# Three of a pair's seven low parts formed in PSUM by a matmul with a negated identity

## The chip, the cores and the metric

The kernel runs on one core of a Trainium2 chip. The metric is the device time of one execution in microseconds (us); shown are the median and the ends of several runs. One further execution was taken by the hardware profiler; its span goes from the first to the last instruction.

## What is computed

One inference step of a small streaming encoder: 1024 prompt tokens and 8 x 16 sample tokens, model width 1024, two layers. Layer 0 has sliding-window attention, layer 1 chunked attention on a shared K/V; each ends in an output projection and an MLP. What matters here, cut from the reference:

```python
def rmsnorm(x, g):
    y = xf * lax.rsqrt(jnp.mean(xf * xf, axis=-1, keepdims=True) + EPS)
    return (y * g.astype(jnp.float32)).astype(x.dtype)

def mlp(x, g_norm, w_up, w_down):
    return jnp.square(jax.nn.relu(rmsnorm(x, g_norm) @ w_up)) @ w_down

        hp = hp + ap @ w_o_a[i]
        hp = hp + mlp(hp, g_mlp[layer], w_up[layer], w_down[layer])
```

All is in float32 and has to be accurate, so the kernel splits each factor of a product into a high and a low part and adds three matmuls.

## The kernel before

**High and low parts.** TensorE multiplies in a shorter format (fp32r). `split` (L107 to L115) writes the high part with a copy that rounds to that format, by ScalarE unless told otherwise (L109), and the low part as source minus high part, by VectorE (L115). A product is three matmuls: high by high, high by low, low by high (L715 to L717 in the MLP, L147 to L149 in the output projection).

**The stage around the change.** `wo_phase` runs once in each layer, between attention and the MLP. It takes the nine tiles of 128 tokens (eight of the prompt, ST of the sample) in the order of WO_ORDER. For each, M(t) adds attention times output weights to x (L653, by VectorE from the bank ps_wo), stores x (L655, a DMA that ScalarE issues) and norms it in place: a square with a sum by ScalarE (L605), two small operations, and the scaling of x by VectorE (L610), which overwrites what the store reads. `load_o` splits attention's output (tiles oh and ol).

**Pairs and parts.** The MLP multiplies 2 x 2 blocks with seven products instead of eight. So as soon as tile i and tile i + 4 are done, S(i) forms four sums and differences of their halves on GpSimd (tiles s; L669 to L672), and T(i) turns seven parts p = 0 to 6, each 128 tokens by 512: the halves x1 low, x1 high, x2 high, then the four sums. There are four pairs in a layer, i = 0 to 3. `turn` transposes a part on TensorE in four pieces into one PSUM bank (ps_n, three banks in turn, L662), ScalarE copies the high part out of it into sx (L109), VectorE subtracts the low part into sx (L115), and the bank is free. The sample's tile is turned in two parts of its own.

**What follows.** `mlp_up` starts with a block of its own kind: the first 256 tokens of each half (pairs 0 and 1) and then the other 256, so that TensorE has products while the last pairs are turned. Its products go 0, 1, 5, ...: the first fills ps_x, which ScalarE copies (hc, L834); the second fills ps_z, which VectorE adds (L836); the third adds to ps_x and is copied (L839), and so on. The block's weights are loaded (ru), combined by VectorE (L775 to L778) and split (w, wq) by the same two engines.

**What sets the order.** Each engine works through its own queue in order. The queues are not written by hand here: a scheduler deals the instructions of the whole program to the queues, by a timeline that it works out and by priorities; the products of the MLP are tied to their order. So a change of one step can deal the instructions around it anew.

Of the kernel before, what the change touches and what calls it, by code (L numbers as in the profile page):

```python
# [9 lines left out]
F32R = mybir.dt.float32r  # L10
AF = mybir.ActivationFunctionType
ALU = mybir.AluOpType
# [4 lines left out]
P = 128  # L17
# [58 lines left out]
class Build:  # L76
# [535 lines left out]
    def wo_phase(self, layer, sx, x8, wo):  # L612
        nc = self.nc
        with ExitStack() as st:
            self.psum_pools(st, f"wo{layer}", dict(m=(4, 1), g=(3, 1)), dict(m="m", n="g"))
            work = self.pool(st, f"wow{layer}")
            small = self.pool(st, f"wosm{layer}", 2)
            osp, xs = {}, {}
            lo, hi = slice(0, 512), slice(512, 1024)

            def O(t, z):
                if t in self.kept:
                    xs[t] = self.kept[t]
                    return
                if len(xs) % 5 < 2:
                    xs[t] = self.rawp.tile([P, D], F32, tag="raw", name="x")
                else:
                    xs[t] = work.tile([P, D], F32, tag="x", name="x", bufs=3)
                nc.sync.dma_start(xs[t], self.xd[t])
                if t in self.wo_done:  # L630
                    return
                with self.tc.high_priority(WO_PRIO) if len(osp) < 2 else nullcontext():
                    load_o(t, z)

            def second():
                self.last = work.tile([P, 4, P], F32, tag="o2", name="o2")
                return self.last

            def load_o(t, z):
                o = work.tile([P, 4, P], F32, tag=f"o{z}", name="o")  # L640
                self.load_halves(layer, 1, t, o, second, nc.vector)
                oh = work.tile([P, 4, P], F32R, tag=f"oh{z}", name="oh")
                ol = work.tile([P, 4, P], F32R, tag=f"ol{z}", name="ol")
                self.split(oh, ol, o)
                osp[t] = oh, ol

            def M(t):
                x = xs[t]
                for n in range(2) if t not in self.wo_done else ():
                    nn = slice(n * 512, n * 512 + 512)  # L650
                    ps = self.psum("m", [P, 512], "ps_wo")
                    self.wo_proj(ps, *osp[t], wo, nn)
                    nc.vector.tensor_tensor(x[:, nn], ps, x[:, nn], ALU.add)  # L653
                if t not in self.wo_done:
                    nc.scalar.dma_start(self.xd[t], x)  # L655
                if t not in self.kept:
                    self.norm(small, work.tile([P, D], mybir.dt.bfloat16, tag="junk", name="junk"), x)

            def turn(src, dst, c, d):
                ps = self.psum("n", [P, 4, P], "ps_n")  # L660
                for k in range(4):
                    nc.tensor.transpose(ps[:, k, :], src[:, k * P : (k + 1) * P], self.ident)  # L662
                self.split(dst[0][:, d, c], dst[1][:, d, c], ps)

            def S(i):
                x1, x2 = xs[i], xs[i + NT // 2]
                s = self.sums() if i else self.sums0
                tt = nc.gpsimd.tensor_tensor
                tt(s[0], x2[:, lo], x2[:, hi], ALU.add)  # L669
                tt(s[1], s[0], x1[:, lo], ALU.subtract)  # L670
                tt(s[2], x1[:, lo], x2[:, lo], ALU.subtract)
                tt(s[3], x1[:, hi], s[1], ALU.subtract)  # L672
                return [x1[:, lo], x1[:, hi], x2[:, hi], *s]

            def T(i, src):
                c = slice(i * P, i * P + P)
                for p in (0, 1, 2, 3, 4, 5, 6):
                    turn(src[p], sx[p], c, slice(0, 4))

            order = WO_ORDER[layer]  # L680
            ready, pend = set(), []
            z = 0
            for t in order[:2]:
                O(t, z % 2)
                z += t not in self.wo_done
            for n, t in enumerate(order):
                if n + 2 < NTILE:
                    O(order[n + 2], z % 2)
                    z += order[n + 2] not in self.wo_done
                M(t)  # L690
                ready.add(t)
                for f in pend:
                    f()
                pend = []
                if t == ST:
                    def sample():
                        for h in range(2):
                            turn(xs[ST][:, h * 512 : h * 512 + 512], x8, slice(0, P), slice(4 * h, 4 * h + 4))
                    pend.append(sample)
                elif (t + 4) % NT in ready:  # L700
                    i = t % 4
                    T(i, S(i))
            for f in pend:
                f()
# [1094 lines left out]
```

## Time and profile before

| | |
|---|---|
| runs | 2407.91 us median of 3 (2406.41 to 2412.36) |
| profiled execution, span | 2399.3 us |
| TensorE / weight loads busy | 2320.4 us (97%) / 1935.5 us (81%) |
| VectorE / ScalarE / GpSimd busy | 1626.3 us (68%) / 1217.9 us (51%) / 535.6 us (22%) |
| mean granted TensorE clock | 0.992 |
| output projection of layer 0 and of layer 1, with the turns | about 397 to 457 us and 1642 to 1692 us |

No time of its own is given for the profiled execution beside its span; the runs were timed apart from it. In the rows of the profile PE is TensorE, PEld its weight loads, DVE VectorE, ACT ScalarE, POOL GpSimd and SP SyncE; L12 is line 12 of the kernel. A row of the timeline has start, length, engine, line, operation, and in brackets the idle time before it with what ended it. A row of the groups has count, busy us, mean ns of one, then the idle time before them. A row of the waits has who waited for whom, us in total, times, and the longest. A row of the stretches has length, then busy us of PE, PEld, DVE, ACT and POOL with the number of instructions, the granted clock, the share of the DMA engines and GB/s.

### The profile page before, as it was taken

The page shows a single profiled execution, that of the slowest core. Times are in us where ns is not written, and L with a number is a line of the kernel's source. Part 1 is how long each engine was busy: PE and PEld are TensorE (multiplying, and loading weights), DVE is VectorE, ACT ScalarE, POOL GpSimd, SP SyncE. Part 2 cuts the span into 40 slices and gives each one's busy share as a digit, 9 for nine tenths or more (in the row PEclk, how much of TensorE's full clock was granted, in tenths as well). Part 3 has the DMA queues.
Part 4 walks back from the last instruction along what each step waited for, and adds up shares of the span by engine and source line. Part 5 has one row for each costly group of instructions (what it writes and reads, how often), then busy time and mean ns, then how long its engine had stood idle before and what let it go on. Part 6 is the DMA issues. An engine that isn't in the chain of part 4 may idle for free.

```text
span 2399.3 us, 33421 instructions
## 1 busy us (share of the span) xinstructions
PE 2320.4 (97%) x11621; PEld 1935.5 (81%) x11621; DVE 1626.3 (68%) x3002; ACT 1217.9 (51%) x2423; POOL 535.6 (22%) x828
## 2 busy tenths in 40 slices
PE   7998999899999999999999999998999999999999
PEld 6786877788888888888777788887888888888887
DVE  6687786755655777776567877877655555776674
ACT  4676675555555433232267666665655555333321
POOL 3343332312112100000333434344211211000000
PEclk9998999999999999999999999999999999999999
DMA  7345546244433874342743555555434435744332
GB/s 244 122 127 168 171 156 200 95 155 158 145 128 141 323 245 146 117 141 99 237 149 111 188 161 173 173 169 174 138 127 145 154 137 200 278 140 158 112 116 114
DMA packets 218457, 385.88 MB, mean 161 GB/s; under 512 B 50408, under 2 KB 125104, under 8 KB 211120
## 3 DMA queue, kind: packets, MB, share of 16 engines
q1 hardware_dynamic: 195136, 307.16, 39.0%
q0 software_dynamic: 21776, 71.84, 7.7%
q10 hardware_dynamic: 1376, 4.74, 0.5%
q8 instruction: 92, 1.51, 0.3%
q14 instruction: 77, 0.63, 0.1%
HBM read 246.47 MB, written 136.14 MB: 159 GB/s over the span
## 4 chain that ended last, share of the span: by engine, by line
PE 82%; DMA 7%; DVE 5%; ACT 2%; issue 2%; POOL 1%; SPq 1%; ACTq 0%; DVEq 0%; POOLq 0%
PE ps_x L715 9%; PE ps_x L717 9%; PE ps_x L716 9%; PE ps_y L717 7%; PE ps_y L716 7%; PE ps_y L715 7%; PE ps_mm L186 3%; PE ps_mm L188 3%; PE ps_mm L187 3%; PE ps_tr L293 2%; PE ps_mm L147 2%; PE ps_mm L149 2%; PE ps_mm L148 2%; PE ps_s L717 1%; PE ps_s L716 1%
## 5 line engine op out<-in xcount | busy, mean ns | idle before, releaser
L109 ACT CAST w<-r 128x2048 fp32r<-128x2048 f32 x56 | 107.1, 1913 | 322.9 <-PE ps_y L717 212.1
L715 PE MATMUL ps_x<-w,s 128*128 128x512 f32 x512 | 199.5, 390 | 2.7 <-DVE hc L854 2.1
L717 PE MATMUL ps_x<-w,s 128*128 128x512 f32 x512 | 199.4, 389 | 0.0
L716 PE MATMUL ps_x<-w,s 128*128 128x512 f32 x512 | 199.2, 389 | 0.0
L186 PE MATMUL ps_mm<-w,hh 128*128 128x512 f32 x432 | 175.0, 407 | 13.8 <-ACT kw L253 5.1
L188 PE MATMUL ps_mm<-w,hl 128*128 128x512 f32 x432 | 174.3, 403 | 1.7 <-DMA hl<-hTd 1.4
L187 PE MATMUL ps_mm<-w,hh 128*128 128x512 f32 x432 | 172.5, 400 | 0.7 <-DVE w L159 0.7
L109 ACT CAST s<-s 128x2048 fp32r<-128x2048 f32 x56 | 107.1, 1913 | 117.9 <-DMA s<-hd 108.6
L115 DVE TENSOR_TENSOR w<-r,w 128x2048 fp32r<-128x2048 f32 x56 | 128.2, 2290 | 51.9 <-ACT w L109 51.9
L715 PE MATMUL ps_x<-sx,w 128*128 128x512 f32 (+1 forms) x408 | 157.8, 387 | 4.6 <-ACT hc L834 2.7
L1021 DVE TENSOR_TENSOR x<-ps_y,x 128x512 f32<-128x512 f32 x136 | 92.3, 687 | 101.1 <-PE ps_y L717 101.0
L717 PE MATMUL ps_x<-sx,w 128*128 128x512 f32 (+1 forms) x408 | 154.1, 378 | 0.0
L716 PE MATMUL ps_x<-sx,w 128*128 128x512 f32 (+1 forms) x408 | 154.1, 378 | 0.0
L109 ACT CAST w<-ru 128x512 fp32r<-128x512 f32 (+1 forms) x160 | 110.0, 708 | 85.3 <-PE ps_y L716 32.0
L717 PE MATMUL ps_y<-w,s 128*128 128x512 f32 x384 | 149.5, 389 | 0.0
L716 PE MATMUL ps_y<-w,s 128*128 128x512 f32 x384 | 149.4, 389 | 0.0
L715 PE MATMUL ps_y<-w,s 128*128 128x512 f32 x384 | 149.4, 389 | 0.0
L115 DVE TENSOR_TENSOR s<-s 128x2048 fp32r<-128x2048 f32 x56 | 128.1, 2287 | 26.5 <-ACT s L109 26.5
L115 DVE TENSOR_TENSOR ptl<-ps_tr,pth 128x512 fp32r<-128x512 f32 x180 | 122.6, 685 | 24.8 <-ACT pth L109 19.0
L115 DVE TENSOR_TENSOR w<-ru,w 128x512 fp32r<-128x512 f32 (+1 forms) x160 | 126.6, 793 | 10.9 <-ACT w L109 10.8
L109 ACT CAST pth<-ps_tr 128x512 fp32r<-128x512 f32 x180 | 104.8, 594 | 47.9 <-PE ps_tr L293 39.3
L115 DVE TENSOR_TENSOR wq<-ru,wq 128x1024 fp32r<-128x1024 f32 x32 | 39.7, 1240 | 131.9 <-ACT wq L109 131.9
(280 smaller groups left out, 6573.3 us busy)
## 6 DMA issues: line engine op xcount, KB each, us to landing
s<-hd SPq DMA_DIRECT2D x56, 1024.0 KB, 4.7
ru<-in_w_up SPq DMA_DIRECT2D x64, 512.0 KB, 3.9
r<-in_w_down SPq DMA_DIRECT2D x32, 1024.0 KB, 5.7
hd<-hc POOLq DMA_DIRECT2D x128, 256.0 KB, 2.7
hd<-hs POOLq DMA_DIRECT2D x96, 256.0 KB, 2.5
x<-xd SPq DMA_DIRECT2D x41, 512.0 KB, 4.6
o<-oTd SPq DMA_DIRECT2D x52, 256.0 KB, 4.1
hTd<-hh SPq DMA_DIRECT2D x36, 256.0 KB, 4.5
```

What stands on the lines that cost most here:

```text
L109: a = nc.scalar.copy(hi, src)
L115: return a, e.tensor_tensor(lo, src, hi.bitcast(F32), ALU.subtract)
L147: nc.tensor.matmul(ps, oh[:, k, :], w[:, 0, k, nn], start=(k == 0), stop=False)
L148: nc.tensor.matmul(ps, oh[:, k, :], w[:, 1, k, nn], start=False, stop=False)
L149: nc.tensor.matmul(ps, ol[:, k, :], w[:, 0, k, nn], start=False, stop=(k == 3))
L186: nc.tensor.matmul(ps, a, w[:, 0, k, :], start=(k == 0), stop=False)
L187: nc.tensor.matmul(ps, a, w[:, 1, k, :], start=False, stop=False)
L188: nc.tensor.matmul(ps, b, w[:, 0, k, :], start=False, stop=(k == KC - 1))
L715: a = mm(ps, ah, bh, start=first, stop=False, skip_group_check=True)
L716: mm(ps, ah, bl, start=False, stop=False, skip_group_check=True)
L717: return a, mm(ps, al, bh, start=False, stop=last, skip_group_check=True)
L1021: tt(xs[t][:, N[n]], ps, xs[t][:, N[n]], ALU.add)
```

## The change

In the pairs i = 1, 2 and 3, the parts p = 1, 3 and 5 get their low part in another way. The four transposes are written as matmuls of an accumulation group that stays open. ScalarE copies the high part as before. Then one matmul with a negated identity (minus, a new tile of 128 x 128 made by VectorE once in each layer) adds minus the high part to the whole bank, so that the bank holds the low part, and ScalarE copies that too. VectorE has no part in these turns. That is 9 of 30 turns in each layer, 18 in all. The first pair and the sample are turned as before.

```diff
+            minus = work.tile([P, P], F32R, tag="minus", name="minus")
+            nc.vector.tensor_scalar(minus, self.ident, -1.0, None, ALU.mult)
...
-            def turn(src, dst, c, d):
+            def turn(src, dst, c, d, scalar=False):
                 ps = self.psum("n", [P, 4, P], "ps_n")
+                hi, lo = dst[0][:, d, c], dst[1][:, d, c]
+                if scalar:
+                    for k in range(4):
+                        nc.tensor.matmul(
+                            ps[:, k, :], src[:, k * P : (k + 1) * P], self.ident,
+                            start=(k == 0), stop=False, is_transpose=True, skip_group_check=True,
+                        )
+                    nc.scalar.copy(hi, ps)
+                    nc.tensor.matmul(ps, minus, hi, start=False, stop=True, skip_group_check=True)
+                    nc.scalar.copy(lo, ps)
+                    return
                 for k in range(4):
                     nc.tensor.transpose(ps[:, k, :], src[:, k * P : (k + 1) * P], self.ident)
-                self.split(dst[0][:, d, c], dst[1][:, d, c], ps)
+                self.split(hi, lo, ps)
...
-                    turn(src[p], sx[p], c, slice(0, 4))
+                    turn(src[p], sx[p], c, slice(0, 4), i and p in (1, 3, 5))
```

In the changed kernel the lines behind it stand 13 lower: the transposes are L675, or L666 in the new turns, their high copy is L670, the new matmul L671, the low copy L672, and the copies hc are L847 and L852 where they were L834 and L839.

The new matmuls move other instructions in each queue. The first place is ScalarE's queue in layer 0 from the norm of the last tile on. Before:

```order
L605 ACTIVATE junk,mssq<-x 128x1024
L109 CAST sx<-ps_n 128x4x128 x5
L109 CAST w<-ru 128x1024
L109 CAST w<-ru 128x512 x2
L109 CAST sx<-ps_n 128x4x128 x3
```

After:

```order
L605 ACTIVATE junk,mssq<-x 128x1024
L672 CAST sx<-ps_n 128x4x128 x2
L109 CAST sx<-ps_n 128x4x128
L670 CAST sx<-ps_n 128x4x128
L109 CAST sx<-ps_n 128x4x128
L672 CAST sx<-ps_n 128x4x128
L109 CAST sx<-ps_n 128x4x128
L670 CAST sx<-ps_n 128x4x128
L109 CAST w<-ru 128x1024
L109 CAST w<-ru 128x512 x2
L109 CAST sx<-ps_n 128x4x128
L672 CAST sx<-ps_n 128x4x128
```

Eight copies of parts stand ahead of the first weight cast where there were five; three of them are low parts. The same queue from there to the first copy of the MLP's sums, before:

```order
L109 CAST w<-ru 128x512
L109 CAST sx<-ps_n 128x4x128
L109 CAST sx<-ps_n 128x512
L109 CAST w<-ru 128x512
L109 CAST sx<-ps_n 128x512
L834 COPY hc<-ps_x 128x256
L109 CAST w<-ru 128x1024
```

After:

```order
L670 CAST sx<-ps_n 128x4x128
L109 CAST sx<-ps_n 128x4x128
L109 CAST w<-ru 128x512
L672 CAST sx<-ps_n 128x4x128
L109 CAST w<-ru 128x512
L670 CAST sx<-ps_n 128x4x128
L109 CAST sx<-ps_n 128x4x128
L109 CAST w<-ru 128x1024
L109 CAST sx<-ps_n 128x512
L672 CAST sx<-ps_n 128x4x128
L109 CAST sx<-ps_n 128x512
L847 COPY hc<-ps_x 128x256
```

The last weight cast now stands ahead of the copy hc, and so do the low copies. From the norm to the copy hc there are 18 copies of parts where there were 11; in layer 1, where the queue is dealt in the same way, 21 where there were 15, and the weight cast is ahead of the copy too. VectorE's queue has two low parts fewer there ahead of the last addition into x (L653).

The second place is TensorE's queue in layer 1 between the first and the second product of the MLP (ps_x and ps_z). Before:

```order
L717 MATMUL ps_x<-sx,wq 128x256
L662 MATMUL ps_n<-identr,x 128x128 x8
L662 MATMUL ps_n<-identr,s 128x128 x16
L662 MATMUL ps_n<-identr,x 128x128 x12
L662 MATMUL ps_n<-identr,s 128x128 x12
L715 MATMUL ps_z<-sx,w 128x256
```

After:

```order
L666 MATMUL ps_n<-identr,x 128x128 x4
L675 MATMUL ps_n<-identr,x 128x128 x4
L666 MATMUL ps_n<-identr,s 128x128 x4
L671 MATMUL ps_n<-sx,minus 128x512 x2
L675 MATMUL ps_n<-identr,s 128x128 x4
L666 MATMUL ps_n<-identr,s 128x128 x4
L675 MATMUL ps_n<-identr,s 128x128 x4
L671 MATMUL ps_n<-sx,minus 128x512
L675 MATMUL ps_n<-identr,x 128x128 x4
L666 MATMUL ps_n<-identr,x 128x128 x4
L675 MATMUL ps_n<-identr,x 128x128 x4
L666 MATMUL ps_n<-identr,s 128x128 x4
```

Each new matmul stands one to three turns behind the transposes of its own part. Elsewhere the queues differ only in the last part of attention in layer 1 (some 240 of TensorE's rows, from the place of the new VectorE instruction on, with three loads of x that SyncE now issues ahead of a store), and by single rows.

## The prediction

> **What bounds the kernel now.** I read the page first, then the busy time by stretch, then the waits of the two stretches in which TensorE is not full, and last the timeline of ScalarE and VectorE there.
>
> ```profile
> span 2399.3 us, 33421 instructions
> PE 2320.4 (97%) x11621; PEld 1935.5 (81%) x11621; DVE 1626.3 (68%) x3002; ACT 1217.9 (51%) x2423; POOL 535.6 (22%) x828
> ```
>
> TensorE is busy for 97% of the span, so only its idle time, 79 us in all, can be won, and only where the change acts. The rows below are stretches: length, then busy us of TensorE, weight loads, VectorE, ScalarE and GpSimd, the granted clock, and the DMA share.
>
> ```profile
> 396.00:440.00 44.00, 44.00 (x230) 36.69 (x228) 32.72 (x48) 19.57 (x34) 21.30 (x19) 1.00 0.50 170
> 440.00:460.00 20.00, 12.66 (x90) 10.18 (x90) 18.57 (x28) 13.61 (x26) 5.59 (x5) 1.00 0.33 111
> 460.00:560.00 100.00, 100.00 (x562) 87.59 (x562) 53.90 (x80) 55.01 (x97) 17.92 (x33) 1.00 0.38 134
> 1560.00:1642.00 82.00, 77.84 (x432) 64.93 (x431) 61.60 (x153) 50.50 (x141) 34.46 (x47) 1.00 0.54 173
> 1642.00:1664.00 22.00, 21.81 (x116) 17.91 (x115) 15.98 (x24) 11.46 (x22) 13.07 (x10) 1.00 0.69 215
> 1664.00:1694.00 30.00, 21.05 (x130) 17.16 (x129) 26.97 (x41) 19.21 (x35) 12.50 (x11) 0.89 0.32 113
> 1694.00:1800.00 106.00, 106.00 (x589) 92.56 (x589) 57.76 (x87) 59.12 (x104) 18.99 (x35) 1.00 0.39 135
> ```
>
> Ahead of each MLP there is one such stretch: 440 to 460 us in layer 0, where TensorE idles 20.00 - 12.66 = 7.3 us, and 1664 to 1694 us in layer 1, where it idles 8.95 us. Before and after them it is full. In both VectorE is the busiest engine (18.57 of 20, 26.97 of 30) and ScalarE has room (6.4 and 10.8 us idle). The waits say the same (us in total, times, longest): first of the whole run, then of the two stretches.
>
> ```profile
> PE ps_n L662 <- DVE sx L115: 9.4, 10, 2.4
> PE ps_n L662 <- DVE sx L115: 3.2, 5, 1.6
> PE ps_n L662 <- DVE sx L115: 6.2, 5, 2.4
> DVE x L610 <- DMA xd<-x: 2.0, 2, 1.0
> ```
>
> All ten waits of the transposes for VectorE's low parts lie in these stretches: three banks hold the transposed parts, and a bank is free only when VectorE has subtracted. So the stretch ends when VectorE has worked through its queue, and that queue is what the change shortens.
>
> **The change part by part.** The groups of the operations that it moves (count, busy us, mean ns), and two neighbouring matmuls of 512 columns:
>
> ```profile
> L115 DVE TENSOR_TENSOR sx<-ps_n,sx 128x512 fp32r<-128x512 f32 x60 | 38.8, 682 | 4.4 <-ACT sx L109 4.0
> L109 ACT CAST sx<-ps_n 128x512 fp32r<-128x512 f32 x60 | 33.6, 588 | 32.2 <-PE ps_n L662 28.7 <-DVE x L653 2.8 <-DMA x<-xd 0.2
> 431.26 0.39 PE L148 MATMUL ps_wo<-w,oh 128*128 128x512 f32 x1
> 431.49 0.39 PE L149 MATMUL ps_wo<-w,ol 128*128 128x512 f32 x1
> 444.77 1.89 DVE L115 TENSOR_TENSOR sx<-ps_n,sx 128x512 fp32r<-128x512 f32 x3 [0.48 <-ACT sx L109]
> ```
>
> *VectorE* loses 18 of the 60 subtractions, nine in each layer. In a run one costs 1.89 / 3 = 0.63 us. In layer 0 six of the nine fall in the stretch, the others earlier where TensorE is full: 6 x 0.63 = 3.8 us come off VectorE's queue. In layer 1 all nine do: 5.7 us.
>
> *TensorE* gains 18 matmuls of 512 columns. The two rows of the timeline start 0.23 us apart, so they cost 18 x 0.23 = 4.1 us of it. Some three in layer 0 stand among the projections before 440 us, where the stretch's VectorE queue still covers them; the rest lie in its idle time (7.3 and 8.95 us). So I count them at nothing. If that cover were gone, they would cost the 4.1 us.
>
> *The bank* of a moved part is held for longer: copy 0.59, matmul 0.39, copy 0.59 instead of copy 0.59 and subtraction 0.68, that is 0.3 us more, with one more hand-over between engines. With six moved parts among three banks this is 0.6 us a layer, and it is late only if the banks are the limit; I leave it inside ScalarE's idle time below.
>
> *ScalarE* gains 18 copies, and this decides the sum, since its queue runs in order and the next stage's work stands in it. The place is the queue from the last norm (L605) to the first copy of the MLP's sums (L834), and on to the second (L839), after which TensorE is full:
>
> ```profile
> 441.39 0.68 DVE L653 TENSOR_TENSOR x<-ps_wo,x 128x512 f32<-128x512 f32 x1
> 442.95 1.06 ACT L605 ACTIVATE junk<-x 128x1024 bf16<-128x1024 f32 x1
> 444.15 1.56 ACT L109 CAST sx<-ps_n 128x512 fp32r<-128x512 f32 x3
> 455.87 0.38 ACT L834 COPY hc<-ps_x 128x256 f32<-128x256 f32 x1
> 456.30 0.39 PE L715 MATMUL ps_x<-sx,w 128*128 128x256 f32 x1 [1.36 <-ACT hc L834]
> 457.01 1.05 ACT L109 CAST w<-ru 128x1024 fp32r<-128x1024 f32 x1 [0.76 <-DMA ru<-in_w_up]
> 457.72 0.28 PE L717 MATMUL ps_x<-sx,w 128*128 128x256 f32 x1
> 458.97 0.35 ACT L839 COPY hc<-ps_x 128x256 f32<-128x256 f32 x1
> 459.38 0.39 PE L715 MATMUL ps_x<-sx,w 128*128 128x256 f32 x1 [1.38 <-ACT hc L839]
> 1673.87 1.06 ACT L605 ACTIVATE junk<-x 128x1024 bf16<-128x1024 f32 x1
> 1690.41 0.38 ACT L834 COPY hc<-ps_x 128x256 f32<-128x256 f32 x1
> 1693.00 0.39 PE L715 MATMUL ps_x<-sx,w 128*128 128x256 f32 x1 [0.46 <-ACT hc L839]
> 442.95:455.87 12.92, 8.98 (x63) 6.70 (x61) 12.17 (x19) 9.98 (x20) 3.77 (x4) 1.00 0.22 73
> 1673.87:1690.41 16.54, 13.19 (x82) 10.43 (x81) 14.78 (x23) 12.43 (x24) 5.96 (x6) 0.89 0.20 70
> ```
>
> The last two rows are stretches again: between norm and copy ScalarE is busy 9.98 of 12.92 us in layer 0 and 12.43 of 16.54 us in layer 1. By the order of instructions seven copies more stand there in layer 0 (six low parts and one high part) and six in layer 1, and in both the weight cast of 1.05 us that stood behind L834 now stands ahead of it. A copy in a run costs 1.56 / 3 = 0.52 us. Layer 0: 9.98 + 7 x 0.52 + 1.05 = 14.67 us, which is 1.75 more than the 12.92 it took. Layer 1: 12.43 + 6 x 0.52 + 1.05 = 16.60 us, 0.06 more than 16.54. That is without any idle time of ScalarE in between. It had 2.9 and 4.1 us; some stays, because each low copy waits for a matmul that itself waits for the high copy. I take 1.2 us in each layer, with 0.5 and 2.0 as ends.
>
> Against that stand two gains. The last norm starts sooner: in layer 0 VectorE has two low parts fewer (1.26 us) ahead of the addition L653 that the norm reads, and ScalarE one copy more (0.52): 0.74 us. In layer 1 one of the two lies ahead of a norm that waits for a store anyway (the wait of L610 for the DMA): 0.63 us. And in layer 0 the weight cast is out of the way between the two copies: from L834 to the next product it took 459.38 - 455.87 = 3.51 us, and without the cast it is 0.43 to the product's start, 1.70 for the product, 0.35 for the copy and some 0.17 in hand-overs, 2.65 us. In layer 1 it was 1693.00 - 1690.41 = 2.59 us, so nothing is won.
>
> Sum: layer 0 1.75 + 1.2 - 0.74 - 0.86 = +1.35 us; layer 1 0.06 + 1.2 - 0.63 + 0.06 = +0.69 us; together +2.0 us, from +0.6 to +3.6 with the idle time's ends.
>
> *The new tile* minus costs one small VectorE instruction in each layer, at the end of attention, with no wait of its own. Its own cost is below one 0.63 us subtraction, and VectorE has 20 us idle between 1560 and 1642. But from there to the end of attention in layer 1 the order of score products, transposes and projections, and of a few loads on SyncE, is dealt anew. TensorE idles 82.00 - 77.84 = 4.2 us there; I put the new deal at 0, with 2 us to either side, half of that idle time.
>
> The sum is made in the span of 2399.3 us. The median of the runs is 2407.91 us, 8.6 us above it; what lies around the span is taken as unchanged. So 2407.9 + 2.0 = **2409.9**, rounded to 2410, and 2406.5 to 2413.5 for this case by itself.
>
> A rule that speaks against the change: the Trainium skill, ScalarE: Activation LUTs, section Rules for kernel authors, tells an author to give plain arithmetic to VectorE and not to ScalarE, because per element VectorE is up to about three times as fast for bf16. By it a moved part would cost ScalarE up to 3 x 0.68 = 2.0 us, the six in each stretch 9 us more than here, and the time would be about 2428. The rows above (588 ns for ScalarE, 682 ns for VectorE, both fp32 from PSUM) do not bear it out for this shape.
>
> **The rivals.**
>
> *VectorE's relief is passed on in full* (faster). For it: VectorE is the busiest engine in both stretches and all ten waits of the transposes name it. Against: ScalarE's queue, with 14.7 us to do in the 12.9 us. It gives 3.8 + 5.7 = 9.5 us, 2398.4.
>
> *TensorE stalls behind the new matmul* (slower). The matmul with minus stands in TensorE's queue and waits for the high copy; transposes and products behind it wait too. If none of this is hidden, each moved part keeps TensorE for 0.59 + 0.39 us: 18 x 0.98 = 17.6 us, less the 9.4 us for which it waits now for VectorE, +8.2: 2416.1. It decides from a mean wait of about 0.5 us for each new matmul (9.4 / 18). For it: in layer 1 the matmul often stands one or two transposes behind its own part. Against: in layer 0 several stand a product or a dozen projections later.
>
> *The clock stays up in layer 1* (forecast less 2.9). TensorE's granted clock falls there, after a gap:
>
> ```profile
> 1666.00:1668.00 2.00, 0.05 (x1) 0.00 (x0) 1.62 (x3) 1.73 (x5) 0.22 (x2) 1.00 0.68 250
> 1668.00:1670.00 2.00, 0.66 (x4) 0.42 (x4) 1.94 (x2) 0.59 (x1) 1.92 (x3) 1.00 0.00 0
> 1670.00:1672.00 2.00, 0.59 (x3) 0.62 (x4) 2.00 (x4) 0.00 (x0) 2.00 (x2) 0.64 0.00 0
> 1672.00:1674.00 2.00, 2.00 (x11) 2.00 (x10) 2.00 (x4) 1.20 (x3) 2.00 (x2) 0.50 0.00 0
> 1674.00:1676.00 2.00, 2.00 (x11) 2.00 (x11) 1.01 (x3) 1.02 (x2) 0.82 (x2) 0.50 0.64 262
> 1676.00:1678.00 2.00, 2.00 (x12) 1.77 (x10) 1.84 (x2) 0.98 (x2) 0.00 (x0) 0.65 0.00 0
> ```
>
> After 4.7 us of idling in 6 the clock is 0.50 to 0.65, and busy time times the missing share is 0.59 x 0.36 + 2 x 0.5 + 2 x 0.5 + 2 x 0.35 = 2.9 us. New matmuls and freer banks could break the gap. The time would be 2407. Against: the norms of VectorE that wait for a store lie in the gap, and they stay. The rule beside it is in the Trainium skill, TensorE: Matmul & The Clock Gate, section Why this matters for your kernels: gaps of TensorE above about 3 us bring the clock back to half; the rows agree, and layer 0, whose longest such wait is 1.6 us, keeps 1.00.
>
> **How the numbers follow.** A measurement of this kernel can tell about 0.3%, 7.2 us, from no change: faster is below 2400.7, slower above 2415.1. Chances: forecast 0.56, relief in full 0.10, stall 0.15, clock kept 0.19. Clock kept and forecast lie within 0.3%, but for a tail of the forecast of 0.01 to each side; of the relief 0.08 counts as faster and of the stall 0.14 as slower. That makes 0.09, 0.76 and 0.15. The range reaches from 2402, which leaves out most of the relief in full, to 2417, which takes in the stall at its price and leaves out worse: about 0.17 outside.
>
> **What would show it.** Right: between 440 and 460 us VectorE falls to about 15 us busy, ScalarE rises to 16 or more, TensorE's idle time stays near 7 us in layer 0 and 9 in layer 1, and its waits name ScalarE's copies in place of VectorE's low parts; the first copy of the MLP's sums comes later after the last norm by about the 1.75 + 1.2 us in layer 0. Wrong: TensorE's idle time in the two stretches below 9 us together (relief), above 23 us (stall), or a difference that begins before 396 us or between 1560 and 1642 us, where only the order was dealt anew.

## The result and the profile after

| | before | after |
|---|---|---|
| median of 20 runs | 2406.03 us (2395.55 to 2412.36) | 2412.95 us (2403.49 to 2420.36) |
| after / before | | 1.0035, 95% interval 1.0024 to 1.0046: +8.4 us (+5.8 to +11.1) |
| profiled execution, span | 2399.3 us | 2411.6 us |
| mean granted clock there | 0.992 | 0.989 |

The median lies in the predicted range, but the change costs about 8 us by the ratio of the runs (the two medians differ by 6.9 us) where 2 were forecast. The page of the changed kernel:

```profile
PE 2329.3 (97%) x11639; PEld 1942.9 (81%) x11639; DVE 1618.8 (67%) x2986; ACT 1225.2 (51%) x2441; POOL 536.5 (22%) x828
```

VectorE lost 7.5 us, ScalarE gained 7.3 us and TensorE 8.9 us of busy time.

To compare kernels I use two stretches that can be found in every trace: from the first matmul of the output projection (L147) to the second product behind a ScalarE copy of the MLP's sums, from which on TensorE is full.

The stretches by engine, before and then after (length, then busy us of TensorE, weight loads, VectorE, ScalarE, GpSimd, and the granted clock):

```profile
397.10:459.40 62.30, 54.96 (x307) 45.30 (x305) 50.66 (x75) 33.18 (x59) 26.89 (x24) 1.00 0.43 150
1644.60:1693.00 48.40, 39.36 (x219) 32.09 (x218) 40.57 (x61) 28.91 (x53) 24.61 (x21) 0.93 0.48 162
```

```profile
400.60:467.00 66.40, 58.37 (x315) 48.02 (x313) 46.97 (x66) 37.49 (x68) 26.94 (x24) 0.97 0.44 150
1653.20:1705.20 52.00, 41.21 (x226) 33.72 (x225) 37.88 (x52) 33.22 (x62) 23.98 (x21) 0.93 0.47 159
```

The stretches are 4.1 and 3.6 us longer, 7.7 together, near the 8.4 of the runs. Each length comes from one execution. In the kernels of the table below whose turns are unchanged in that layer and that have three banks, layer 0 took 62.3 to 62.6 us and layer 1 took 47.0 to 49.0, so a difference below 2 us in layer 1 says little.

VectorE is relieved by 6.4 us, and TensorE gets nothing of it: its busy time grows by 5.3 us, 4.1 of them the new matmuls as the prediction counted them, and its idle time does not shrink but grows, from 110.70 - 94.32 = 16.4 to 118.40 - 99.58 = 18.8 us (sums of the two rows). In layer 0 VectorE lost 3.7 us and ScalarE gained 4.3.

The spans differ by 12.3 us, since the profiled execution of before was a quick one. Of the 4.6 us outside the stretches, 1.0 lies between them and 3.5 us lie ahead of the first, at the end of attention in layer 0, where loads of its output came late in the execution of after (between 375 and 392 us):

```profile
ACT oh L109 <- DMA o<-oTd: 4.0, 2, 2.6
...
PE ps_mm L147 <- DVE xo L1521: 1.9, 1, 1.9
```

That is not of the change: the same wait stands in the executions of e6 (1.79 us) and of e12 (2.50 us) below, both without it.

What TensorE waited for, changed kernel, first the stretch of layer 0, then that of layer 1:

```profile
PE ps_n L675 <- DVE sx L115: 3.3, 3, 1.5
PE ps_x L728 <- ACT hc L847: 2.0, 1, 2.0
PE ps_n L666 <- ACT sx L672: 0.9, 2, 0.6
PE ps_n L675 <- ACT sx L672: 0.5, 1, 0.5
...
PE ps_n L666 <- DVE sx L115: 0.4, 1, 0.4
...
PE ps_n L671 <- ACT sx L670: 0.3, 1, 0.3
...
PE ps_n L666 <- DVE sx L115: 2.3, 2, 2.1
PE ps_x L728 <- ACT hc L847: 2.2, 1, 2.2
PE ps_wo L147 <- ACT oh L109: 1.7, 1, 1.7
PE ps_n L675 <- DVE sx L115: 1.2, 2, 0.7
PE ps_n L675 <- ACT sx L672: 1.1, 2, 0.8
PE ps_n L671 <- ACT sx L670: 1.0, 3, 0.5
...
PE ps_n L666 <- ACT sx L672: 0.2, 1, 0.2
```

L666 are the transposes of a moved part, L671 its matmul, L670 and L672 ScalarE's two copies, L675 the transposes of the other parts. Before, the transposes waited 9.4 us, all for VectorE. Now they wait 3.3 + 0.4 + 2.3 + 1.2 = 7.2 us for VectorE and 0.9 + 0.5 + 0.3 + 1.1 + 1.0 + 0.2 = 4.0 us for ScalarE's copies: 11.2 us. So the relief of VectorE won 2.2 us of waits, and the moved parts brought 4.0 new ones and 4.1 us of matmuls.

One row in layer 1 does not belong to the turns: a projection (L147) waits 1.7 us for the split of attention's output (oh), since an addition of VectorE ahead of the split (L310) ran 1.77 us while GpSimd formed a sum. In e3, which has the same change in that layer, the addition took 0.69 us and this wait is 0.5, and the stretch is 1.2 us shorter than the 52.0. So by this comparison about 1.2 of layer 1's 3.6 us are not the cost of the moved parts.

### The profile page after: what moved, and what is told of

The parts are those of the page before. It is cut to its first block, busy times and chain, and to the rows that moved or that the text cites. A ratio compares the mean times of both kernels' runs of the same rounds, so it can differ in the third digit from the quotient of the medians.

```text
span 2411.6 us, 33461 instructions
## 1 busy us (share of the span) xinstructions
PE 2329.3 (97%) x11639; PEld 1942.9 (81%) x11639; DVE 1618.8 (67%) x2986; ACT 1225.2 (51%) x2441; POOL 536.5 (22%) x828
## 4 chain that ended last, share of the span: by engine, by line
PE 80%; DMA 8%; DVE 5%; ACT 3%; issue 1%; SPq 1%; POOL 1%; ACTq 0%; DVEq 0%; POOLq 0%
PE ps_x L728 9%; PE ps_x L730 9%; PE ps_x L729 9%; PE ps_y L730 7%; PE ps_y L728 7%; PE ps_y L729 7%; PE ps_mm L186 3%; PE ps_mm L188 3%; PE ps_mm L187 3%; PE ps_tr L293 2%; PE ps_mm L147 2%; PE ps_mm L149 2%; PE ps_mm L148 2%; PE ps_s L730 1%; PE ps_s L729 1%
## 5 line engine op out<-in xcount | busy, mean ns | idle before, releaser
L728 PE MATMUL ps_x<-sx,w 128*128 128x512 f32 (+1 forms) x408 | 159.6, 391 | 5.1 <-ACT hc L847 4.2
L115 DVE TENSOR_TENSOR w<-r,w 128x2048 fp32r<-128x2048 f32 x56 | 128.2, 2290 | 51.7 <-ACT w L109 51.7
L729 PE MATMUL ps_x<-sx,w 128*128 128x512 f32 (+1 forms) x408 | 155.7, 382 | 0.0
L730 PE MATMUL ps_x<-sx,w 128*128 128x512 f32 (+1 forms) x408 | 155.6, 381 | 0.0
L109 ACT CAST w<-ru 128x512 fp32r<-128x512 f32 (+1 forms) x160 | 110.1, 708 | 82.9 <-PE ps_y L729 32.0
```

What stands on the lines that cost most here:

```text
L109: a = nc.scalar.copy(hi, src)
L115: return a, e.tensor_tensor(lo, src, hi.bitcast(F32), ALU.subtract)
L728: a = mm(ps, ah, bh, start=first, stop=False, skip_group_check=True)
L729: mm(ps, ah, bl, start=False, stop=False, skip_group_check=True)
L730: return a, mm(ps, al, bh, start=False, stop=last, skip_group_check=True)
```

## The experiments

The first theory, from the two traces: ScalarE's queue, longer by the low copies, holds back the first copy of the MLP's sums (L847). Its rivals: the new deal of instructions upstream; the new matmul with the longer hold of its bank; TensorE standing behind the new matmul. The table gives the two stretches from each profiled execution (us), what their sum is more than 110.1 (the mean of before, 110.7, and of e1, 109.5), and the ratio of the runs to those of before with its 95% interval. Each ratio rests on 20 to 35 runs of before and 5 to 12 of the other kernel (20 of after).

| kernel | layer 0 | layer 1 | sum | ratio of the runs | in us |
|---|---|---|---|---|---|
| before | 62.3 | 48.4 | +0.6 | | |
| after | 66.4 | 52.0 | +8.3 | 1.0035 (1.0024 to 1.0046) | +8.4 |
| e1 minus only | 62.5 | 47.0 | -0.6 | 0.9993 (0.9981 to 1.0005) | -1.7 |
| e2 layer 0 only | 66.7 | 49.0 | +5.6 | 1.0045 (1.0030 to 1.0060) | +10.8 |
| e3 layer 1 only | 62.6 | 50.8 | +3.3 | 1.0014 (1.0000 to 1.0028) | +3.4 |
| e4 low copy by VectorE | 68.8 | 50.4 | +9.1 | 1.0050 (1.0032 to 1.0067) | +12.0 |
| e5 four banks | 63.3 | 47.6 | +0.8 | 1.0015 (1.0001 to 1.0028) | +3.6 |
| e6 before, four banks | 62.9 | 47.0 | -0.2 | 0.9987 (0.9972 to 1.0001) | -3.1 |
| e12 before, four banks, again | 62.9 | 46.7 | -0.5 | 0.9997 (0.9985 to 1.0010) | -0.7 |
| e7 extra copy | 74.0 | 66.0 | +29.9 | 1.0112 (1.0096 to 1.0127) | +26.9 |
| e8 extra matmul | 61.6 | 51.7 | +3.2 | 1.0035 (1.0022 to 1.0049) | +8.4 |
| e9 pair 1 only | 63.2 | 52.2 | +5.3 | 1.0023 (1.0011 to 1.0034) | +5.5 |
| e10 pair 3 only | 63.6 | 50.0 | +3.5 | 1.0011 (0.9997 to 1.0026) | +2.6 |
| e11 four banks, pair 1 | 62.7 | 46.9 | -0.5 | 0.9992 (0.9980 to 1.0005) | -1.9 |

**The tile alone (e1).**

```diff
-                turn(src[p], sx[p], c, slice(0, 4), i and p in (1, 3, 5))
+                turn(src[p], sx[p], c, slice(0, 4), False)
```

> The tile minus is made, and no part is moved: all low parts by VectorE, no new matmul, no new copy. ScalarE's queue ahead of the MLP is as in the kernel before; only the end of attention in layer 1 is dealt anew. Theory (ScalarE's queue holds the MLP's first copy back): 0 +- 2 us against before, ratio 1.000. Rival 1 (the new deal of the order upstream costs the time): most of the 8 us, ratio 1.002 or more. Rival 2 (the new matmul holds banks and TensorE): 0, as the theory.

Measured: 0.9993. With minus made and nothing moved, the end of attention in layer 1 is dealt anew, and nothing is lost: the new deal upstream is ruled out as the cause.

**One layer at a time (e2, and e3 with layer == 1).**

```diff
-                turn(src[p], sx[p], c, slice(0, 4), i and p in (1, 3, 5))
+                turn(src[p], sx[p], c, slice(0, 4), layer == 0 and i and p in (1, 3, 5))
```

> Parts 1, 3 and 5 are moved in layer 0 alone. Theory: layer 0's share. By the two profiles the first copy of the MLP's sums came 2.9 us later after the last norm, and the next product 3.84 instead of 3.51 us later, so +3 to +4.5 us against before, ratio 1.0012 to 1.0019. Rival 1 (the new deal upstream in layer 1): here as much as with minus alone. Rival 2 (new matmul): about half of the whole, 4 us.

> Parts 1, 3 and 5 are moved in layer 1 alone. Theory: layer 1's share: the first copy came 18.6 instead of 16.5 us after the last norm, so +2 to +4 us against before, ratio 1.0008 to 1.0017; with layer 0's share it should sum to the whole. Rival 1: as with minus alone. Rival 2: about 4 us.

Measured: 1.0045 and 1.0014. Both layers pay. The stretch of layer 0 is 66.7 us with the change there and 62.6 us without it, as in the kernels after (66.4) and before (62.3); that of layer 1 is 50.8 with it and 49.0 without. The ratio of e2 lies above the 1.0012 to 1.0019 expected of it. Its runs lost more than its stretches show, 10.8 (7.2 to 14.4) against 5.6 us, and the two layers' ratios add up to more than the whole; the stretches add up roughly, 4.4 + 2.4 us against 7.7.

**The low copy by VectorE (e4).**

```diff
-                    nc.scalar.copy(lo, ps)
+                    nc.vector.tensor_copy(lo, ps)
```

> The high part is still taken off in PSUM by the new matmul, but VectorE makes the copy of the low part. ScalarE's queue is as in the kernel before, the new matmul and the longer hold of the bank stay, VectorE has a copy instead of a subtraction. Theory: the cost goes, 0 +- 2 us against before. Rival 2 (the new matmul and the hold of its bank): it stays, +6 to +9 us, ratio 1.0025 or more. Rival 1: as with minus alone.

Measured: 1.0050. The cost does not go, although ScalarE has no copy more than before. So the low copies in ScalarE's queue cannot be the cause by themselves, and the first theory falls in that form. The order of ScalarE's queue is not cleared by it: in layer 0 of e4 the last weight cast stands ahead of the copy hc, as in the changed kernel. The row of TensorE at the longest wait, and then VectorE's rows:

```profile
449.40 1.12 PE L666 MATMUL ps_n<-identr,x 128*128 128x128 f32 x4 [2.48 <-DVE sx L672]
```

```profile
446.46 2.28 DVE L610 SCALAR_TENSOR_TENSOR x<-x,mrs,gb 128x1024 f32<-128x1024 f32 x1 [0.39 <-POOL mrs L609]
448.66 0.68 DVE L672 CAST sx<-ps_n 128x512 fp32r<-128x512 f32 x1
```

A low part that has to wait for its matmul comes into VectorE's queue behind the scaling of the last tile (2.28 us), and the bank stays taken meanwhile: TensorE idles 2.48 us for it. Whichever engine copies, the part holds its bank until two more steps are through.

**Four banks (e5, and the kernel before with four: e6, e12).**

```diff
-            self.psum_pools(st, f"wo{layer}", dict(m=(4, 1), g=(3, 1)), dict(m="m", n="g"))
+            self.psum_pools(st, f"wo{layer}", dict(m=(4, 1), g=(4, 1)), dict(m="m", n="g"))
```

> The changed kernel with four banks instead of three for the transposed parts. Bank theory (a moved part holds its bank until the new matmul and one more copy are through, so the later parts' transposes come late): most of the cost goes, -1 to +4 us against before, and at most 3 us over the kernel before with four banks. ScalarE theory (its queue holds back the MLP's first copy): the copies are as many as before, +6 to +10 us against before.

> The kernel before with four banks for the transposed parts: the control to the run above. If the three banks bind here too, as the ten waits of the transposes for VectorE (9.4 us) say, -3 to -8 us against before; if VectorE's queue binds and the banks only pass it on, 0 +- 2 us.

> The kernel before with four banks, once more, since its first interval reached from 0.9972 to 1.0001. If the banks bind: the two together below 1.0000, at -2 to -5 us against before. If not: around 0, and the first result was the spread of the runs.

Measured: 1.0015 for e5, 0.9987 and 0.9997 for the control. The stretches of e5 (those of e6, 62.9 and 47.0 us, are in the table):

```profile
396.70:460.00 63.30, 58.08 (x322) 48.78 (x321) 46.53 (x66) 36.52 (x68) 25.82 (x24) 0.97 0.45 159
1648.50:1696.10 47.60, 38.59 (x227) 32.13 (x226) 37.32 (x52) 32.76 (x62) 25.75 (x21) 0.96 0.49 167
```

With a fourth bank the same 18 matmuls and 18 copies lengthen the stretches by 0.4 and 0.6 us against e6 in place of 4.1 and 3.6: TensorE's idle time in layer 0 is 63.30 - 58.08 = 5.2 us instead of 8.0. That fits the bank theory, but does not prove it. The order is dealt anew with the fourth bank, and in e5 the last weight cast stands behind the copy hc again in both layers.

The whole runs say less. Against before the cost falls from 8.4 to 3.6 us (0.2 to 6.7), as the theory expected. Against the kernel before with four banks, e5 stands 6.7 us (e6) or 4.3 us (e12) higher, and at most 3 were expected. By the two traces e5 took 4.5 us longer than e6, of which 1.0 lies in the stretches. So that a fourth bank takes most of the cost away is seen in the stretches of single executions, and the runs do not confirm it.

For the kernel before, the fourth bank wins nothing that its two runs of the test agree on, and each interval reaches 1.0000. What TensorE waited for in layer 0 of e6:

```profile
PE ps_x L715 <- ACT w L109: 1.8, 1, 1.8
PE ps_x L717 <- DVE w L115: 1.6, 1, 1.6
PE ps_n L662 <- DVE sx L115: 1.1, 2, 0.8
```

The transposes' waits for VectorE fall from 3.2 to 1.1 us there (and from 6.2 to 4.0 in layer 1), but the first product now waits 3.4 us for its weights: with a bank more the wait moves on.

**ScalarE's copies alone (e7).**

```diff
                 self.split(hi, lo, ps)
+                if scalar:
+                    nc.scalar.copy(work.tile([P, D], mybir.dt.bfloat16, tag="junk", name="junk")[:, :512], hi.bitcast(F32))
```

> The 18 parts keep VectorE's subtraction and get no new matmul; ScalarE makes one more copy for each, of the high part in SBUF into a tile that nobody reads. So ScalarE's queue is as long as in the changed kernel, and VectorE is not relieved. ScalarE theory: +6 to +12 us against before (the cost, and no relief to set against it). Bank theory: 0 to +3 us.

Measured: 1.0112, over what either theory gave. One row of ScalarE tells why this can't be read:

```profile
452.34 1.06 ACT L605 ACTIVATE junk<-x 128x1024 bf16<-128x1024 f32 x1
```

The copy writes the tile that the norm's square writes, and the scheduler dealt the norms late: the last one starts 21.7 us after the last projection, where before it was 3.4 us. It is the price of that order, not of 18 copies. Inconclusive.

**The matmul alone (e8).**

```diff
+            self.psum_pools(st, f"wo{layer}", dict(m=(4, 1), g=(3, 1), e=(1, 1)), dict(m="m", n="g", e="e"))
...
                 self.split(hi, lo, ps)
+                if scalar:
+                    nc.tensor.matmul(self.psum("e", [P, 4, P], "ps_e"), minus, hi, start=True, stop=True)
```

> The 18 parts keep VectorE's subtraction; the new matmul is made too, but into a bank of its own that nobody reads. So TensorE has the new matmuls and their waits for the high copies in its queue, and the parts' banks are held no longer than before. Bank theory: 0 to +2 us against before. Rival (TensorE stalls behind the new matmul): +5 to +9 us, with waits of L668 for ScalarE of 0.5 us each.

Measured: 1.0035, what the rival said. But its place was another. The stretch of layer 0 in e8, and the wait of the new matmul in that of layer 1:

```profile
397.60:459.20 61.60, 57.15 (x316) 46.83 (x314) 49.50 (x75) 32.35 (x58) 25.97 (x24) 1.00 0.43 150
```

```profile
PE ps_e L668 <- ACT sx L109: 0.7, 1, 0.7
```

In layer 0 the nine matmuls are hidden, as the prediction had it: TensorE is busy 2.2 us more and idle 4.45 instead of 7.3 us, and the stretch is no longer than before. In layer 1 they are not: +3.3 us, of which 1.7 is the late projection that the profiles of the kernel after and of e4 show too. The new matmul itself waits 0.7 us, once. So TensorE does not stand behind it. Of the runs' 8.4 us the two stretches hold 3.2. In the trace of e8 the time between the stretches is 1197.0 us where before it was 1185.2, but it is also 1191.0 us in e1, whose runs lose nothing. So the other 5 us are not explained.

**Which pair (e9, and e10 with i == 3), and pair 1 with four banks (e11: the edits of e9 and e5).**

```diff
-                turn(src[p], sx[p], c, slice(0, 4), i and p in (1, 3, 5))
+                turn(src[p], sx[p], c, slice(0, 4), i == 1 and p in (1, 3, 5))
```

> Parts 1, 3 and 5 of pair 1 alone are moved, three in each layer. In layer 0 their matmuls stand among the projections, before the stretch in which the banks are short. Theory now (a moved part costs where the transposes wait for banks, by the matmul and by waits for ScalarE's copies): -2 to +2 us against before, ratio 0.9992 to 1.0008. Rival (every moved part costs the same, since its matmul and its copy do): a third of the cost, +2.8 us.

> Parts 1, 3 and 5 of pair 3 alone are moved, the last pair of each layer, wholly inside the stretches. Theory now: +3 to +6 us against before, ratio 1.0012 to 1.0025, more than with pair 1 alone. Rival (the same for every part): +2.8 us, the same as with pair 1 alone.

> Four banks for the transposed parts and only pair 1's parts moved. If the two act one by one: the kernel before with four banks (-3.4 us against before) and what pair 1 alone costs or wins, so -5 to 0 us. A version below both kernels if it comes to -4 us or less.

Measured: 1.0023, 1.0011 and 0.9992. My expectation for e9 failed: pair 1 alone costs as much as pair 3 alone or more, and e10 lies just below its 1.0012 to 1.0025. In layer 0 both are small (63.2 and 63.6 us); in layer 1 three moved parts cost as much as nine (52.2 and 50.0). With four banks (e11) pair 1's parts cost nothing in the stretches: 62.7 and 46.9 us, as in e6 and e12. ScalarE's rows of e9 in layer 1 show what is common to the long stretches:

```profile
1695.46 1.04 ACT L109 CAST w<-ru 128x1024 fp32r<-128x1024 f32 x1 [0.80 <-DMA ru<-in_w_up]
...
1696.88 0.38 ACT L847 COPY hc<-ps_x 128x256 f32<-128x256 f32 x1
...
1700.22 0.37 ACT L852 COPY hc<-ps_x 128x256 f32<-128x256 f32 x1 [0.58 <-PE ps_x L730]
```

and the same place in the kernel before:

```profile
1690.94 1.05 ACT L109 CAST w<-ru 128x1024 fp32r<-128x1024 f32 x1
1692.58 0.37 ACT L839 COPY hc<-ps_x 128x256 f32<-128x256 f32 x1 [0.58 <-PE ps_x L717]
```

Before, the first copy (at 1690.41) stands ahead of the weight cast, and the second follows it 2.17 us later. In e9 the cast, with a wait of 0.80 us for its load, stands ahead of the first copy, and the second copy comes 3.34 us after the first. Both second copies wait 0.58 us for the product between the two, so that the product sets the 3.34 us: it ran at half clock in e9, with matmuls 0.21 us apart instead of 0.12.

The cast's place and the half clock go together in every kernel here with three banks. In layer 1 the cast stands ahead of the first copy in after, e3, e9 and e10 (50.0 to 52.2 us), and not in before, e1, e2 (47.0 to 49.0), e4 and e8 (50.4 and 51.7, of which the late projection takes 1.7). In layer 0 it stands ahead in after, e2, e4 and e10 (63.6 to 68.8), and not in before, e1, e3, e8 and e9 (61.6 to 63.2). In e7 it stands ahead in both. Wherever it stands ahead, the next product ran at half clock (in e10's layer 0 from its sixth matmul on), and nowhere else. With four banks this does not hold: in layer 0 of e5 the product ran at half clock with the cast behind the copy. By the rows of e9 this place is worth at most 1.05 + 0.8 us for the cast and its wait and 1.2 us for the slow product, 3.05 of the 3.8 us by which the stretch is longer than before. So the place of the cast is a rival to the bank, and e5 and e11 do not separate the two, since a fourth bank moved the cast too. It is read from the order and was not tried by itself: a kernel that takes only this cast off ScalarE would tell.

No version beats the kernel before by more than its interval. e11 comes nearest, 0.9992 (0.9980 to 1.0005).

## Why the prediction was right in its range and wrong in its size

The direction was right: no relief came through to the time, and more than it was lost. But the sum of +2.0 us was mis-sized, and with its own ends, +0.6 to +3.6, it did not reach the +8.4 of the runs or the +7.7 of the stretches. That the median fell into the stated range is in part luck: the range was made wide for the rivals and the new deal, and it started from a median of three runs that was 1.9 us above that of twenty. The sum's steps against these rows, first VectorE's scaling of the tile before the last, in the kernel before:

```profile
439.59 1.28 DVE L610 SCALAR_TENSOR_TENSOR x<-x,mrs,gb 128x1024 f32<-128x1024 f32 x1 [0.95 <-POOL mrs L609]
```

and then the changed kernel, VectorE with one row of GpSimd, ScalarE and TensorE:

```profile
442.18 1.98 DVE L610 SCALAR_TENSOR_TENSOR x<-x,mrs,gb 128x1024 f32<-128x1024 f32 x1 [1.00 <-DMA xd<-x]
444.08 1.27 DVE L115 TENSOR_TENSOR sx<-ps_n,sx 128x512 fp32r<-128x512 f32 x2
445.27 0.68 DVE L655 TENSOR_TENSOR x<-ps_wo,x 128x512 f32<-128x512 f32 x1
441.78 1.29 POOL L685 TENSOR_TENSOR s<-x,s 128x512 f32<-128x512 f32 x1
```

```profile
447.31 1.07 ACT L605 ACTIVATE junk<-x 128x1024 bf16<-128x1024 f32 x1
...
463.17 0.40 ACT L847 COPY hc<-ps_x 128x256 f32<-128x256 f32 x1
466.59 0.37 ACT L852 COPY hc<-ps_x 128x256 f32<-128x256 f32 x1 [1.06 <-PE ps_x L730]
...
1682.91 1.07 ACT L605 ACTIVATE junk<-x 128x1024 bf16<-128x1024 f32 x1
...
1701.45 0.38 ACT L847 COPY hc<-ps_x 128x256 f32<-128x256 f32 x1
1704.85 0.37 ACT L852 COPY hc<-ps_x 128x256 f32<-128x256 f32 x1 [0.64 <-PE ps_x L730]
```

```profile
463.62 0.58 PE L728 MATMUL ps_x<-sx,w 128*128 128x256 f32 x1 [2.00 <-ACT hc L847]
464.00 0.41 PE L729 MATMUL ps_x<-sx,w 128*128 128x256 f32 x1
464.22 0.41 PE L730 MATMUL ps_x<-sx,w 128*128 128x256 f32 x1
...
467.01 0.58 PE L728 MATMUL ps_x<-sx,w 128*128 128x256 f32 x1 [0.46 <-ACT hc L852]
...
1705.28 0.38 PE L728 MATMUL ps_x<-sx,w 128*128 128x256 f32 x1 [0.46 <-ACT hc L852]
```

- **From the last norm to the first copy.** Layer 0: 463.17 - 447.31 = 15.86 us, 2.94 more than 12.92; forecast 1.75 + 1.2 = 2.95. Right. Layer 1: 1701.45 - 1682.91 = 18.54, 2.0 more than 16.54; forecast 1.26. The size was off by 0.7.
- **"The last norm starts sooner."** Failed. From the first projection it came 46.7 us later instead of 45.9 in layer 0 (+0.9, forecast -0.74), and 29.7 instead of 29.3 in layer 1 (+0.4, forecast -0.63). In layer 0 VectorE's relief did reach the scaling L610 ahead of it, which started 41.6 us after the first projection instead of 42.5. Its wait is no longer either, 1.00 us for a store where it was 0.95 us for GpSimd. But it ran 1.98 us instead of 1.28, while GpSimd formed a sum (L685), and in the new order two low parts and not one stand between it and the addition L655: 3.09 us from the scaling to the addition instead of 1.80. ScalarE's extra copy adds the rest, 0.5 us. In layer 1 the norm is later mainly by the late projection: in e3, without most of that, it came 28.6 us after the first projection. But it came after 28.2 us in e1, where no part is moved, so no gain is seen there.
- **"From the copy to the next product 2.65 us."** Failed: 467.01 - 463.17 = 3.84 in layer 0 (3.51 before; forecast -0.86) and 3.83 in layer 1 (2.59 before; forecast +0.06). The cast left the place between the two copies, as forecast. But in both layers the product between them ran at half clock: in layer 0 its matmuls start 0.22 us apart, where before the twelve from 456.30 to 457.72 started 0.13 apart. From its first matmul to the copy behind it took 466.59 - 463.62 = 2.97 us, and 1.70 was put in for it. ScalarE was not what held that copy back: it waited 1.06 and 0.64 us for the product. The sum had no term for the clock.
- These three terms make +2.94 + 0.86 + 0.33 = +4.1 us in layer 0 and +2.0 + 0.4 + 1.24 = +3.6 us in layer 1, which are the stretches' differences. Of the nearly 6 us that the forecast missed, about 2.7 are the norm that did not start sooner, 2.4 the two products at half clock, and 0.7 the first copy in layer 1.
- **"So I count them at nothing", and the bank "left inside ScalarE's idle time".** This step failed too. Much of TensorE's idle time was waits for banks, and a moved part adds to just those: 4.0 us of waits for ScalarE's copies of parts, which before did not appear. As a plain addition of work the nine matmuls of layer 0 did vanish from the stretch (e8). As a step between a part's copy and its bank's release they did not, and with one bank more the stretches were short again (e5). How much of the cost is the bank and how much the order in ScalarE's queue, with the clock behind it, stays open in both layers.
- **Layer 0 "keeps 1.00" of the clock.** True of the kernel before; in the changed kernel it fell, as the rows below show. The prediction also says that its rows of layer 1 agree with a limit of about 3 us for a gap. They do not quite: the idling there was two waits of 2.33 and 2.38 us with a turn's transposes between them.
- **Its own signs.** VectorE's and ScalarE's busy time and TensorE's idle time (8.0 and 10.8 us) came near what was said, and the copy came later by the 2.95 us. But TensorE's waits name VectorE's low parts still, for 7.2 of 11.2 us.
- **The rivals.** The relief in full did not come. The stall was priced near the result, at 2416, but its mechanism is not what happened: L671 waits 0.3 + 1.0 us in the two stretches, less than 0.1 us for each new matmul where 0.5 was the point of decision. The clock was not kept up in layer 1: 0.93 in that stretch before and after.
- **What was counted at nothing upstream** (tile, new deal) cost nothing: e1.
- **The 8.6 us around the span** were not there. The profiled execution of after has a time of its own, 2413.33 us, 1.7 above its span. By that, the profiled execution of before took 2401.0 us, a quick one among runs of 2395.55 to 2412.36, and the median of three that the forecast started from was 1.9 us above that of twenty.

## What to carry to other kernels

Idle time of an engine can take in extra work only if that work is not on the chain that makes it idle; ask for each idle row what it waits for, and whether the new step stands between that thing's start and its release. Where a ring of few buffers ties engines together, a step that moves work to an idle engine but adds one hand-over to a buffer's life can cost more than it relieves; count the hold of the buffer, and try one buffer more beside the edit. What is won in one engine's queue can be lost again in the same queue, when the steps are dealt in another order or run slower beside another engine. And a stage that lets TensorE wait a little longer can lose its clock: look at the granted clock of the products behind the stage, not only at the waits.

## What the runs showed of the hardware

**The clock fell without a long gap.** Stretches of 2 us of the changed kernel at the start of layer 0's MLP (columns as above; the clock is the third number from the end):

```profile
457.00:459.00 2.00, 1.08 (x8) 0.61 (x7) 2.00 (x4) 1.90 (x4) 0.00 (x0) 1.00 0.34 64
459.00:461.00 2.00, 1.29 (x10) 0.89 (x9) 1.63 (x3) 1.39 (x4) 0.00 (x0) 1.00 0.59 202
461.00:463.00 2.00, 0.62 (x4) 0.39 (x4) 1.13 (x1) 2.00 (x4) 0.00 (x0) 0.89 0.87 251
463.00:465.00 2.00, 1.38 (x6) 1.38 (x7) 1.63 (x4) 0.91 (x3) 0.00 (x0) 0.50 1.05 394
...
467.00:469.00 2.00, 1.99 (x9) 1.99 (x10) 0.00 (x0) 0.00 (x0) 0.00 (x0) 0.50 0.00 0
```

The longest wait there is 2.00 us, and the clock was at half for some 7 us from shortly before its end. The Trainium skill, TensorE: Matmul & The Clock Gate, section Why this matters for your kernels, names gaps above about 3 us. Here 2.00 us were enough, in 6 us in which TensorE was busy for 1.08 + 1.29 + 0.62 = 3.0 us and that mostly with transposes; before, with a longest such wait of 1.6 us, it did not fall. But the longest wait is not what decides: in layer 0 of e2 none is above 1.4 us, and the clock fell there twice. A wait of e2 and two of its stretches of 2 us:

```profile
PE ps_n L675 <- DVE sx L115: 3.2, 3, 1.4
454.00:456.00 2.00, 2.00 (x10) 1.82 (x9) 2.00 (x4) 1.98 (x5) 0.10 (x1) 0.50 0.00 0
464.00:466.00 2.00, 1.76 (x8) 1.76 (x9) 1.24 (x3) 0.88 (x3) 0.00 (x0) 0.52 1.06 373
```

What does decide, these runs do not show. Such waits can cost more than themselves: in the changed kernel the products behind them ran at 0.22 us a matmul instead of 0.13 until about 469 us.

**VectorE's scaling ran slower beside GpSimd.** L610 on 128x1024 took 1.28 us in the row of before above, where GpSimd formed no sum, and 1.98 us beside L685 in the changed kernel; in e4 it took 2.28 us with two sums of GpSimd beside it. The addition L310 took 0.69 us in e3, where it started just ahead of a sum of GpSimd, and 1.77 us in the changed kernel, where it started just behind one.

**A copy out of PSUM by VectorE took as long as the subtraction**, 0.68 us for 128x512 in e4, so taking the second operand away relieves VectorE of nothing.
